# Layer 0's weight products divided as 274, 270 and 272 columns

## The chip, the cores and the metric

The kernel runs on one core of a Trainium2 chip. Its time is the device time of one launch in microseconds; the median of 3 runs of the kernel before is 2330.63 us (2329.7 to 2330.78). The profile is one execution of the same program, recorded by the hardware profiler. TensorE is called PE there (PEld is its weight load), VectorE DVE, ScalarE ACT, GpSimd POOL, SyncE SP.

## The reference

A decoder trunk of two layers, float32 throughout: 16 learned tokens and 256 input tokens make T = 272 tokens of D = 2048 features.

```python
for layer in range(2):
    a = rms_norm(h, norm_attn[layer])
    if layer == 0:
        q, k, v, f = split(a @ fox_w_in)            # 3*2048 + 16 columns
        h = h + forgetting_attention(q, k, v, cumsum(log_sigmoid(f + b_f))) @ fox_w_o
    else:
        k_s, v_s = split(rms_norm(h, kv_norm) @ w_kv)
        h = h + stick_breaking_attention(a @ sb_w_q, k_s, v_s) @ sb_w_o
    h = h + square(relu(rms_norm(h, norm_mlp[layer]) @ w_up[layer])) @ w_down[layer]
return rms_norm(h, final_norm)[:, 16:]
```

`w_up` and `w_down` are 2048 x 8192 and 8192 x 2048. Only the last 256 tokens are returned, so from layer 1's query projection on the kernel leaves out the first 16; the shared K/V projection still takes all 272.

## The kernel before

**Layout.** Features lie on the 128 partitions, tokens along the free dimension. The stream `hT` is [128, 16 chunks of features, 272 tokens] in float32.

**Precision by splitting.** A float32 product is made from rounded products (type F32R). Each weight block is split into a rounded high part `whi` (ScalarE, L222) and the rest `wlo` (VectorE, L223); each activation chunk into `hi` (L138) and `lo` (L139). A weight tile of 128 x 128 takes part in three products, whi x hi, whi x lo and wlo x hi (L253 to L255), accumulated in float32.

**Where the split activations lie.** Class `Split` (L118) takes a buffer of 16 rows, one for each chunk, of `XROW` = 640 columns, and places the two parts in each row by `ROWS` (L27): for T = 272 tokens (`t0` = 0, called layer 0 here, with the shared K/V projection) the high part at column 48 and the low part at 368; for the 256 tokens of layer 1 (`t0` = M) the high part at 304 and the low part at 0. Layer 1 reads low and high part as one operand of 2 x 256 columns (`both`, L132) in one product of 512 columns with `whi` and adds a product of 256 columns with `wlo`. 2 x 272 columns are over the 512 that one accumulator holds, so layer 0 makes three products of 272.

**The product loop.** `gemm_group` (L186) makes 512 output features from 2048 input features: four accumulators of [128, 512] in four banks (`acc`, one for each 128 output features, index m), four blocks kb of 512 input features, each in two halves hf of two tiles kc. The weights of a block are loaded in two transfers by SyncE, then split. In blocks 0 and 3 TensorE goes accumulator by accumulator, four tiles each, 12 products; in blocks 1 and 2 half by half and in it accumulator by accumulator. So a new group takes the accumulators up in the order in which the old group has finished them. The loop's products keep the order written (`gemm_matmul`, L178, pins each behind the one before, but for the first group, whose products follow the loads). The four accumulator buffers are the only ones: each must be evicted before the next group's first product on it.

**Eviction.** After block 3, `evac(m, [accumulator])` is called for each m (L258): q, k and v are scaled by the norm's factor (L376, L380); the output projection (`out_proj`) and the down projection add into `hT` (L262), the former and the last quarter of the latter also split and square the result for the next norm; the up projection makes squared ReLU and splits it (L506 to L510).

**Order.** The order on each engine is made when the program is built, by a scheduler that simulates a timeline; TensorE's is pinned as said. Small attention work of TensorE stands between the groups' products.

**Groups.** With 272 tokens: 12 for q, k, v, 4 for the output projection, 16 up, 16 down, 8 for K/V, 56 in all, of 4 x 16 weight tiles. With 256 tokens: 4, 4, 16 and 16.

Of the kernel before, what the change touches and what calls it, by code (L numbers as in the profile page):

```python
# [9 lines left out]
F32 = mybir.dt.float32  # L10
F32R = mybir.dt.float32r
AF = mybir.ActivationFunctionType
ALU = mybir.AluOpType
AX = mybir.AxisListType

P = 128
D = 2048
NC = D // P
M = 16
# [4 lines left out]
QSCALE = 1.0 / math.sqrt(P)  # L24
N_FF = 4

ROWS = {0: (48, 368), M: (304, 0)}  # L27
XROW = 640

G_A0, G_M0, G_KV, G_A1, G_M1, G_FIN = range(6)  # L30
# [3 lines left out]
def yoco_kernel(ctx: ExitStack, tc: tile.TileContext, hT_in, gains, b_f, w_f, w_qkv0, w_o0, w_up, w_dn,  # L34
                w_kv, w_q1, w_o1, outT):
    nc = tc.nc
# [7 lines left out]
    tmp = ctx.enter_context(tc.tile_pool(name="tmp", bufs=2))  # L44
# [73 lines left out]
    class Split:  # L118


        def __init__(self, label, t0):
            n = T - t0
            self.t0 = t0
            rows = xs.tile([P, NC * XROW + 64], F32R, tag="x", name=f"x_{label}")
            hi, lo = ROWS[t0]
            o = min(hi, lo)
            rows = rows[:, o:o + NC * XROW].rearrange("p (c t) -> p c t", c=NC)
            self.hi, self.lo = (rows[:, :, k - o:k - o + n] for k in (hi, lo))

            d = abs(lo - hi)  # L130
            if t0:
                self.both = rows[:, :, :2 * d].rearrange("p c (i t) -> p c i t", i=2)[:, :, :, :n]  # L132
            self.low_first = lo < hi
# [44 lines left out]
    def gemm_matmul(*args, **kw):  # L178

        ins = nc.tensor.matmul(*args, **kw).ins  # L180
        if queued and pinned[0]:
            tc.add_manual_dep(ins, queued[0].name, mybir.DependencyInfo(mybir.DependencyClass.NoSync,
                                                                        mybir.DependencyReason.DATA))
        queued[:] = [ins]

    def gemm_group(wblk, sp, t0, evac, before={}, after={}, load_x=None, pairs=False, apart=()):  # L186

        uid[0] += 1
        u = uid[0]
        accs = [pacc.tile([P, 512], F32, tag="acc", name=f"acc_{u}_{m}") for m in range(4)]
        n = T - t0
        for kb in range(4):
            src_w = wblk[kb].rearrange("p (k c) -> p k c", k=4)
            if kb in before:
                before[kb]()
            piece = 1 if load_x is not None and kb < 2 else 2  # L200
            raws = [wraw.tile([P, 2, 512], F32, tag="raw", name=f"raw_{u}_{kb}_{hf}") for hf in range(2)]
            for k0 in range(0, 4, piece):
                if load_x is not None:
                    load_x(range(4 * kb + k0, 4 * kb + k0 + piece))
                if load_x is not None and kb == k0 == 0:

                    for c0 in (0, 256):
                        nc.scalar.dma_start(raws[0][:, 0, c0:c0 + 256], src_w[:, 0, c0:c0 + 256])
                else:
                    nc.sync.dma_start(raws[k0 // 2][:, k0 % 2:k0 % 2 + piece], src_w[:, k0:k0 + piece])  # L210
            parts = []
            for hf in range(2):
                whi = wspl.tile([P, 2, 512], F32R, tag="whi", name=f"whi_{u}_{kb}_{hf}")
                wlo = wspl.tile([P, 2, 576], F32R, tag="wlo", name=f"wlo_{u}_{kb}_{hf}")
                wlo = wlo[:, :, 32:544] if pairs else wlo[:, :, :512]
                boxes = [(o, piece, 0, 512) for o in range(0, 2, piece)]
                if load_x is not None and kb == hf == 0:
                    boxes[:1] = [(0, 1, 0, 256), (0, 1, 256, 512)]
                for o, no, c0, c1 in boxes:
                    src = raws[hf][:, o:o + no, c0:c1]  # L220
                    hp, lp = whi[:, o:o + no, c0:c1], wlo[:, o:o + no, c0:c1]
                    on_act = nc.scalar.activation(hp, src, AF.Copy)  # L222
                    on_dve = nc.vector.tensor_tensor(out=lp, in0=src, in1=hp.bitcast(F32), op=ALU.subtract)  # L223
                parts.append((whi, wlo))
            if kb in after:
                with tc.issue_after(on_act.ins), tc.issue_after(on_dve.ins):
                    after[kb]()


            if load_x is not None and kb == 0:  # L230
                runs = [([kc], range(4)) for kc in range(4)]
            elif kb in (0, 3):
                runs = [(range(4), [m]) for m in range(4)]
            else:
                runs = [(range(2 * hf, 2 * hf + 2), range(4)) for hf in range(2)]
            pinned[0] = load_x is None
            for kcs, ms in runs:
                paired = [m for m in ms if pairs and m not in apart]
                single = [m for m in ms if m not in paired]
                for kc in kcs:  # L240
                    for m in paired:
                        gemm_matmul(accs[m], parts[kc // 2][0][:, kc % 2, m * P:(m + 1) * P], sp.both[:, 4 * kb + kc],
                                    start=kb == kc == 0, stop=False)
                for kc in kcs:
                    for m in paired:
                        gemm_matmul(accs[m][:, n:] if sp.low_first else accs[m][:, :n],
                                    parts[kc // 2][1][:, kc % 2, m * P:(m + 1) * P],
                                    sp.hi[:, 4 * kb + kc], start=False, stop=kb == kc == 3)
                for m in single:
                    for kc in kcs:  # L250
                        wh, wl = (w[:, kc % 2, m * P:(m + 1) * P] for w in parts[kc // 2])
                        hi, lo = sp.hi[:, 4 * kb + kc], sp.lo[:, 4 * kb + kc]
                        gemm_matmul(accs[m][:, :n], wh, hi, start=kb == kc == 0, stop=False)  # L253
                        gemm_matmul(accs[m][:, :n], wh, lo, start=False, stop=False)
                        gemm_matmul(accs[m][:, :n], wl, hi, start=False, stop=kb == kc == 3)  # L255
                if kb == 3:
                    for m in ms:
                        evac(m, [accs[m][:, :n]] + ([accs[m][:, n:]] if m in paired else []))  # L258

    def residual_add(c, acc, t0):  # L260
# [16 lines left out]
    def load_x(chunks):  # L277
        c0, n = chunks[0], len(chunks)
        nc.sync.dma_start(hT[:, c0:c0 + n, :], hT_in[:, c0:c0 + n, :])
        if c0 == 0:  # L280
            nc.sync.dma_start(g_sb, gains)
        for c in chunks:
            split_chunk(xa, G_A0, c)
# [86 lines left out]
    for g in range(4):  # L370
# [11 lines left out]
        if g == 0:  # L382

            gemm_group(w_qkv0[0], xa, 0, lambda m, acc, qT=qT: nc.scalar.copy(qT[:, m, :], acc[0]),
                       after={kb: (lambda kb=kb: first_norm(kb)) for kb in range(4)}, load_x=load_x)
            gate_products()
            box["rstd"] = norm.finish()
            for m in range(4):
                evac_q(m, [qT[:, m, :]])
            forget_gates(box["rstd"])  # L390
        else:
            gemm_group(w_qkv0[3 * g], xa, 0, evac_q)
# [4 lines left out]
        def decays(j):  # L397

            for i, (o, n) in enumerate(((0, 144), (144, T))):
                nc.vector.scalar_tensor_tensor(out=s[:, j, o:o + n], in0=fk[:, j, :n],  # L400
                                               scalar=fq_sb[:, i, 4 * g + j:4 * g + j + 1],
                                               in1=maskA[:, o:o + n], op0=ALU.subtract, op1=ALU.add)

        gemm_group(w_qkv0[3 * g + 1], xa, 0, lambda m, acc: evac_kv(m, acc, kT),
                   after={j: (lambda j=j: decays(j)) for j in range(4)})

# [31 lines left out]
        for pr in range(2):  # L438
            pp_sb = att.tile([P, 2, 416], F32, tag="pp", bufs=3, name=f"pp_sb_{g}_{pr}")
            for i in range(2):  # L440
# [14 lines left out]
                                in0=pm[:, P - M:P].unsqueeze(1).to_broadcast([P, 8, M]))  # L455
# [98 lines left out]
    for g in range(4):  # L554
# [30 lines left out]
        for pr in range(2):  # L585
# [3 lines left out]
            for i in range(2):  # L589
# [4 lines left out]
                                    in1=maskB[:, 0:256].unsqueeze(1).to_broadcast([P, 2, 256]))  # L594
            nc.vector.tensor_tensor(out=zp[:, :, 256:400], in0=pb[:, :, :144], op=ALU.add,
                                    in1=maskB[:, 256:400].unsqueeze(1).to_broadcast([P, 2, 144]))
# [15 lines left out]
            for t in (240, 384):  # L612
                nc.vector.tensor_tensor(out=zp[:, :, t:t + M], in0=zp[:, :, t:t + M],
                                        in1=sc[:, 2 * pr:2 * pr + 2, :], op=ALU.add)
# [57 lines left out]
    for i in range(2):  # L672
        pr = patt.tile([P, 512], F32, tag="patt", name=f"pr_fin_{i}")
        for b in range(2):
            nc.tensor.matmul(pr[:, b * P:(b + 1) * P], rs[:, b:b + 1].to_broadcast([P, P]), ident,
                             start=True, stop=True)
# [4 lines left out]
    for c, n in [(12, 1), (13, 1), (14, 1), (15, 1), (0, 2), (2, 2), (4, 2), (6, 2)]:  # L681
        if n == 1:
            nc.vector.scalar_tensor_tensor(out=ob[:, c, :S], in0=hT[:, c, M:], scalar=g_sb[:, G_FIN, c:c + 1],
                                           in1=prs[0], op0=ALU.mult, op1=ALU.mult)
        else:
            nc.vector.tensor_tensor(out=ob[:, c:c + n, :S], in0=hT[:, c:c + n, M:], op=ALU.mult,  # L686
                                    in1=prs[0].unsqueeze(1).to_broadcast([P, n, S]))
        nc.sync.dma_start(outT[:, c:c + n, :], ob[:, c:c + n, :S])
    for c in (8, 10):
        nc.gpsimd.tensor_tensor(out=ob[:, c:c + 2, :S], in0=hT[:, c:c + 2, M:], op=ALU.mult,  # L690
                                in1=pr_sb.unsqueeze(1).to_broadcast([P, 2, S]))
# [52 lines left out]
```

## Time and profile before

| | |
|---|---|
| median of 3 runs | 2330.63 us |
| span of the profiled execution | 2330.1 us |
| products on TensorE | 16486 |
| VectorE, ScalarE busy | 1351.1 us, 1064.1 us |
| from HBM | 407.29 MB, 176 GB/s over the span |

The head of the profile gives each engine's busy time; the chain of waits follows the work that ended last back to the start; the view of stretches gives, for a piece of the span, each engine's busy time and, in brackets, the number of its instructions; the timeline lists instructions by start, merged where neighbours are alike. A group's row reads: line, engine, operation, output <- inputs, shapes, count | busy us, mean ns of one | idle time before it.

### The profile page before, as it was taken

What the parts mean: (1) busy time and instruction counts of PE and PEld (TensorE: products, weight loads), DVE (VectorE), ACT (ScalarE), POOL (GpSimd) and SP (SyncE); (2) the same over time, 40 slices, a digit from 0 to 9 for tenths busy, and PEclk for the clock granted to TensorE, in tenths of its full rate; (3) what the DMA queues carried; (4) which work ended last, traced back from release to release, by engine and by line L of the source; (5) the groups of instructions that cost most, each with busy time, mean ns of one, the idle gap of its engine ahead of it and who ended that gap; (6) DMA issues with size and microseconds to landing.
All of it is one profiled execution on the core that took longest, in us unless ns stands there. A gap on an engine that the chain in (4) does not pass through costs nothing.

```text
span 2330.1 us, 39954 instructions
## 1 busy us (share of the span) xinstructions
PE 2317.9 (99%) x16486; PEld 2197.0 (94%) x16486; DVE 1351.1 (58%) x1923; ACT 1064.1 (46%) x1477; POOL 39.1 (2%) x58
## 2 busy tenths in 40 slices
PE   9999999999999999999999999999999999999998
PEld 9999999999999999999998999988888888888887
DVE  7665555655455455455566555567665665665665
ACT  5434344543354344344455444445544543543553
POOL 1000000000000000000000000000000000000000
PEclk9999999999999999999999999999999999999999
DMA  6445545555555555555555444455555656556563
GB/s 232 165 157 169 168 159 172 172 182 172 186 174 182 173 183 171 186 176 177 184 176 188 163 145 145 145 180 182 197 181 185 198 181 198 182 187 196 181 197 127
DMA packets 116630, 412.00 MB, mean 177 GB/s; under 512 B 13264, under 2 KB 16736, under 8 KB 116448
## 3 DMA queue, kind: packets, MB, share of 16 engines
q1 hardware_dynamic: 114560, 406.29, 52.6%
q10 hardware_dynamic: 1888, 3.16, 0.4%
q8 instruction: 129, 2.11, 0.4%
q14 instruction: 53, 0.43, 0.1%
HBM read 407.29 MB, written 2.11 MB: 176 GB/s over the span
## 4 chain that ended last, share of the span: by engine, by line
PE 99%; DMA 1%; DVE 0%; ACT 0%; issue 0%; DVEq 0%; ACTq 0%; SPq 0%
PE acc L180 95%; DMA hT<-hT_in 1%; PE ps L412 0%; PE pza L591 0%; PE pv L345 0%; PE po L474 0%; PE po L630 0%; PE pzb L592 0%; PE po L631 0%; DMA g_sb<-gains 0%; PE po L475 0%; PE po L632 0%; DVE ob L686 0%; PE pf L311 0%; PE pf L312 0%; PE pta L606 0%
## 5 line engine op out<-in xcount | busy, mean ns | idle before, releaser
L223 DVE TENSOR_TENSOR wlo<-raw,whi 128x1024 fp32r<-128x1024 f32 (+1 forms) x773 | 931.7, 1217 | 752.3 <-ACT whi L222 750.8
L222 ACT ACTIVATE whi<-raw 128x1024 fp32r<-128x1024 f32 (+1 forms) x773 | 799.0, 1050 | 960.8 <-PE acc L180 938.2
L180 PE MATMUL acc<-x_u,whi 128*128 128x272 f32 (+2 forms) x3088 | 648.2, 321 | 0.0
L180 PE MATMUL acc<-x_m,whi 128*128 128x272 f32 (+1 forms) x3072 | 646.7, 322 | 0.0
L180 PEld LDWEIGHTS acc<-x_u,whi 128*128 128x128 f32 x3088 | 500.5, 188 | 26.5
L180 PEld LDWEIGHTS acc<-x_m,whi 128*128 128x128 f32 x3072 | 498.6, 188 | 27.2
L180 PE MATMUL acc<-x_u,wlo 128*128 128x272 f32 (+1 forms) x2048 | 448.1, 284 | 0.0
L180 PE MATMUL acc<-x_m,wlo 128*128 128x272 f32 (+1 forms) x2048 | 446.0, 284 | 0.0
L180 PE MATMUL acc<-x_a,whi 128*128 128x272 f32 (+1 forms) x1792 | 361.1, 306 | 1.4 <-ACT whi L222 1.2
L180 PEld LDWEIGHTS acc<-x_u,wlo 128*128 128x128 f32 x2048 | 342.1, 188 | 16.2
L180 PEld LDWEIGHTS acc<-x_m,wlo 128*128 128x128 f32 x2048 | 341.4, 188 | 16.4
L180 PEld LDWEIGHTS acc<-x_a,whi 128*128 128x128 f32 x1792 | 284.7, 189 | 10.7 <-ACT whi L222 1.6
L180 PE MATMUL acc<-x_a,wlo 128*128 128x272 f32 (+1 forms) x1024 | 255.1, 287 | 0.0
L180 PE MATMUL acc<-x_kv,whi 128*128 128x272 f32 x1024 | 194.1, 288 | 0.0
L180 PEld LDWEIGHTS acc<-x_a,wlo 128*128 128x128 f32 x1024 | 180.1, 188 | 5.0 <-issue 0.5
L180 PE MATMUL acc<-x_o,whi 128*128 128x272 f32 (+1 forms) x768 | 162.5, 322 | 0.0
L180 PEld LDWEIGHTS acc<-x_kv,whi 128*128 128x128 f32 x1024 | 160.6, 188 | 0.4
L180 PE MATMUL acc<-x_kv,wlo 128*128 128x272 f32 x512 | 147.3, 288 | 0.0
L262 DVE TENSOR_TENSOR hT<-acc,hT 128x256 f32<-128x256 f32 (+1 forms) x239 | 102.5, 429 | 72.0 <-PE acc L180 70.1
L180 PEld LDWEIGHTS acc<-x_o,whi 128*128 128x128 f32 x768 | 124.4, 188 | 6.7
L180 PE MATMUL acc<-x_o,wlo 128*128 128x272 f32 (+1 forms) x512 | 112.1, 284 | 0.0
L180 PEld LDWEIGHTS acc<-x_kv,wlo 128*128 128x128 f32 x512 | 96.5, 188 | 0.1
(226 smaller groups left out, 1040.2 us busy)
## 6 DMA issues: line engine op xcount, KB each, us to landing
raw<-w_up SPq DMA_DIRECT2D x256, 512.0 KB, 4.7
raw<-w_dn SPq DMA_DIRECT2D x256, 512.0 KB, 4.8
raw<-w_qkv SPq DMA_DIRECT2D x92, 512.0 KB, 3.8
raw<-w_o SPq DMA_DIRECT2D x64, 512.0 KB, 4.5
raw<-w_kv SPq DMA_DIRECT2D x64, 512.0 KB, 3.7
raw<-w_q SPq DMA_DIRECT2D x32, 512.0 KB, 4.6
fk<-f_dram ACTq DMA_DIRECT2D x4, 544.0 KB, 4.8
raw<-w_qkv SPq DMA_DIRECT2D x7, 256.0 KB, 4.5
```

The lines of the kernel that those rows point to most:

```text
L180: ins = nc.tensor.matmul(*args, **kw).ins
L222: on_act = nc.scalar.activation(hp, src, AF.Copy)
L223: on_dve = nc.vector.tensor_tensor(out=lp, in0=src, in1=hp.bitcast(F32), op=ALU.subtract)
L262: nc.vector.tensor_tensor(out=hT[:, c, t0:], in0=a, in1=hT[:, c, t0:], op=ALU.add)
```

## The change

In layer 0 the high and low parts of a chunk are put side by side, columns 48 to 320 and 320 to 592 of a row. The view `last_lo` begins two columns ahead of the low part, so it holds the high part of the last two tokens and then the low part of all 272. The three products of a weight tile become:

- whi x `last_lo`, 274 columns, into columns 0 to 274 of the accumulator,
- whi x the high part of the first 270 tokens, into columns 2 to 272,
- wlo x the high part of all 272 tokens, into columns 2 to 274.

Columns 2 to 274 then hold the tokens, and columns 0 and 1 the product of `whi` with the high part of the last two tokens. At eviction these two columns are copied by ScalarE to a small tile `over` and added by VectorE to columns 272 and 273, in place, before `evac` gets columns 2 to 274.

```diff
-ROWS = {0: (48, 368), M: (304, 0)}
+ROWS = {0: (48, 320), M: (304, 0)}
+OVER = 2
...
+            if not t0:
+                self.last_lo = rows[:, :, n - OVER:2 * n]
...
-                        gemm_matmul(accs[m][:, :n], wh, hi, start=kb == kc == 0, stop=False)
-                        gemm_matmul(accs[m][:, :n], wh, lo, start=False, stop=False)
-                        gemm_matmul(accs[m][:, :n], wl, hi, start=False, stop=kb == kc == 3)
+                        if t0 == 0:
+                            gemm_matmul(accs[m][:, :OVER + n], wh, sp.last_lo[:, 4 * kb + kc],
+                                        start=kb == kc == 0, stop=False)
+                            gemm_matmul(accs[m][:, OVER:n], wh, hi[:, :n - OVER], start=False, stop=False)
+                            gemm_matmul(accs[m][:, OVER:OVER + n], wl, hi, start=False, stop=kb == kc == 3)
+                        else:
...
                 if kb == 3:
                     for m in ms:
+                        if t0 == 0:
+                            last = accs[m][:, n:n + OVER]
+                            over = tmp.tile([P, OVER], F32, tag="over", name=f"over_{u}_{m}")
+                            nc.scalar.copy(over, accs[m][:, :OVER])
+                            nc.vector.tensor_tensor(out=last, in0=last, in1=over, op=ALU.add)
+                            evac(m, [accs[m][:, OVER:OVER + n]])
+                            continue
```

The `else` branch holds the three products of before, for layer 1.

More of the change, by code (lines that the diff above doesn't have):

```diff
@@ L252, in gemm_group @@
                         hi, lo = sp.hi[:, 4 * kb + kc], sp.lo[:, 4 * kb + kc]
-                        gemm_matmul(accs[m][:, :n], wh, hi, start=kb == kc == 0, stop=False)
-                        gemm_matmul(accs[m][:, :n], wh, lo, start=False, stop=False)
-                        gemm_matmul(accs[m][:, :n], wl, hi, start=False, stop=kb == kc == 3)
+                        if t0 == 0:
[4 more added lines that the diff above has]
+                        else:
+                            gemm_matmul(accs[m][:, :n], wh, hi, start=kb == kc == 0, stop=False)
+                            gemm_matmul(accs[m][:, :n], wh, lo, start=False, stop=False)
+                            gemm_matmul(accs[m][:, :n], wl, hi, start=False, stop=kb == kc == 3)
                 if kb == 3:
                     for m in ms:
+                        if t0 == 0:
[5 more added lines that the diff above has]
+                            continue
                         evac(m, [accs[m][:, :n]] + ([accs[m][:, n:]] if m in paired else []))
```

## The prediction

> **What bounds the kernel now.** I read the head of the profile first, then its chain of waits, then what TensorE waited for, then stretches of the span.
>
> ```profile
> span 2330.1 us, 39954 instructions
> PE 2317.9 (99%) x16486; PEld 2197.0 (94%) x16486; DVE 1351.1 (58%) x1923; ACT 1064.1 (46%) x1477; POOL 39.1 (2%) x58
> ...
> PE 99%; DMA 1%; DVE 0%; ACT 0%; issue 0%; DVEq 0%; ACTq 0%; SPq 0%
> ```
>
> 99% of the chain that ends last is TensorE. The other engines matter only where they make TensorE wait. How often that is, the view of TensorE's waits says (who waited for whom: total us, times, longest):
>
> ```profile
> PE pr_fin L675 <- DVE fin L669: 1.3, 1, 1.3
> PE acc L180 <- ACT whi L222: 1.2, 2, 0.9
> PE idle L61 <- DVE mean_w L57: 1.1, 1, 1.1
> ```
>
> These are the costliest three, and they come to under 4 us. So the time is the number of products times the distance between the starts of two of them. "Busy" means little here (a busy engine may still be slow), hence the view of stretches, which counts the products that start in each:
>
> ```profile
> core 0: us, PE busy (x) PEld busy (x) DVE busy (x) ACT busy (x) POOL busy (x), PEclk, DMA share, GB/s
> 444.00:1190.00 746.00, 746.00 (x6049) 745.95 (x6048) 389.16 (x475) 320.73 (x411) 0.00 (x0) 1.00 0.54 178
> ```
>
> From 444 to 1190 us layer 0 runs nothing but 272-column products at full granted clock (PEclk 1.00): 746 us / 6049 = 123.33 ns each, 370.0 ns for the three of one weight tile, 0.4534 ns a column. No wait interrupts them. The number of weight tiles that the change touches is the number of `wlo` products of 272 columns, in the view of groups with shapes kept apart:
>
> ```profile
> L180 PE MATMUL acc<-x_m,wlo 128*128 128x272 f32 x1024 | 293.4, 287 | 0.0
> L180 PE MATMUL acc<-x_u,wlo 128*128 128x272 f32 x1024 | 293.4, 286 | 0.0
> L180 PE MATMUL acc<-x_a,wlo 128*128 128x272 f32 x768 | 216.9, 289 | 0.0
> L180 PE MATMUL acc<-x_kv,wlo 128*128 128x272 f32 x512 | 147.3, 288 | 0.0
> L180 PE MATMUL acc<-x_o,wlo 128*128 128x272 f32 x256 | 73.6, 288 | 0.0
> ```
>
> 1024 + 1024 + 768 + 512 + 256 = 3584 tiles (the shared K/V projection is among them), 3584 × 0.370 = 1326 us of the span. One ns more or less per tile is 3.6 us, 0.15%. (The 287 ns in these rows is one product from start to end; products overlap, so it is not the pace.)
>
> **The change, part by part.**
>
> *Products.* Three products stay three, with a weight load each, and 274 + 270 + 272 = 816 columns are as many as 3 × 272. If a column costs the same wherever it stands, the pace stays at 370.0 ns. It need not. The first product now starts two columns ahead of a chunk's low part, at column 318 of its row, where every stream of before starts at a multiple of 16 columns (48, 368, 304, 0); two of the three outputs start at column 2 of their bank; the low part moves up against the high part. The trace has no such product, so I bound the price per column by other rows. Layer 1 alternates products of 512 columns (two pieces of 256, a gap between them) with products of 256. First its usual pace, then a stretch of its last group, both from the timeline (start us, us, engine, line):
>
> ```profile
> 1606.62 2.01 PE L180 MATMUL acc<-x_m,whi 128*128 128x512 f32 x8
> 1608.47 1.11 PE L180 MATMUL acc<-x_m,wlo 128*128 128x256 f32 x8
> 1609.41 2.01 PE L180 MATMUL acc<-x_m,whi 128*128 128x512 f32 x8
> ...
> 2308.08 1.53 PE L180 MATMUL acc<-x_u,whi 128*128 128x512 f32 x6
> 2309.45 0.84 PE L180 MATMUL acc<-x_u,wlo 128*128 128x256 f32 x6
> 2310.12 0.28 PE L180 MATMUL acc<-x_u,whi 128*128 128x256 f32 x1
> ```
>
> 8 × (512 + 256) = 6144 columns in 1609.41 − 1606.62 = 2.79 us is 0.4541 ns a column; 6 × 768 = 4608 columns in 2310.12 − 2308.08 = 2.04 us is 0.4427. The same shapes run at two paces, so columns alone don't set it. The dearest row is in layer 1's attention, products of the same rounded type read in two pieces each:
>
> ```profile
> 1335.46 0.40 PE L607 MATMUL pta<-el,ntri_r 128*128 128x512 f32 x1
> 1335.69 0.29 PE L608 MATMUL pta<-eh,nones_r 128*128 128x288 f32 x1
> 1335.83 0.30 PE L609 MATMUL pta<-el,nones_r 128*128 128x288 f32 x1
> 1335.96 0.29 PE L611 MATMUL ptb<-el,ntri_r 128*128 128x288 f32 x1
> 1336.09 0.41 PE L180 MATMUL acc<-x_kv,whi 128*128 128x272 f32 x2
> ```
>
> 512 + 3 × 288 = 1376 columns in 0.63 us: 0.4578 ns a column. For 816 columns the three prices give 361.2, 370.5 and 373.6 ns against 370.0: −31 us, +2 us and +13 us over 3584 tiles. The new first product is in substance a scrap of 2 columns and a run of 272, nearest to the rows that read two pieces, so I take the middle of the two dearer ones: 0.45595 × 816 = 372.1 ns, +2.1 ns a tile, **+7.3 us**. The ends stay −31 and +13.
>
> The Trainium skill ("SBUF — State Buffer", Door 1: The DMA port swizzle) says that SBUF has 16-byte lines and that each access that crosses to a new line pays something; it names no price. Column 318 lies 8 bytes past such a line, so by that rule the first product touches one line more than 272 aligned columns and the sum goes up, never down; no run here shows it.
>
> *Eviction.* 56 groups × 4 accumulators get one copy on ScalarE and one add on VectorE, 128x2 each. Ops of that size stand in the final normalisation:
>
> ```profile
> L664 ACT ACTIVATE fin<-fin 128x2 f32<-128x2 f32 x1 | 0.2, 204 | 0.9 <-DVE fin L663 0.9
> L667 DVE TENSOR_TENSOR fin<-fin 128x2 f32<-128x2 f32 x1 | 0.2, 160 | 0.5 <-ACT fin L665 0.5
> ```
>
> 224 × 0.204 = 46 us of ScalarE and 224 × 0.160 = 36 us of VectorE, on engines that are 46% and 58% busy. They are free while each accumulator is evicted before TensorE wants it again. Accumulator m is wanted 36 products after its last one (three accumulators of 12 products lie between), 36 × 0.1233 = 4.44 us later. The tightest is the fourth. In the changed program its copy stands behind both splits `whi` of the next block on ScalarE; on VectorE its add stands behind both `wlo`, and in the groups that also feed a norm (four of the output projection) its eviction behind one correction and one sum of squares as well. The timeline of a group with norm work in the kernel before:
>
> ```profile
> 1117.92 1.06 ACT L222 ACTIVATE whi<-raw 128x1024 fp32r<-128x1024 f32 x1 [0.84 <-ACT sq_a L155]
> 1118.74 0.44 DVE L262 TENSOR_TENSOR hT<-acc,hT 128x272 f32<-128x272 f32 x1 [0.69 <-PE acc L180]
> 1119.61 1.04 ACT L222 ACTIVATE whi<-raw 128x1024 fp32r<-128x1024 f32 x1
> 1120.23 0.48 DVE L139 SCALAR_TENSOR_TENSOR x_a<-hT,g_sb,x_a 128x256 fp32r<-128x256 f32 x1
> 1120.62 0.44 DVE L156 TENSOR_TENSOR ssq_a<-ssq_a,sq_a 128x272 f32<-128x272 f32 x1
> 1120.98 1.22 DVE L223 TENSOR_TENSOR wlo<-raw,whi 128x1024 fp32r<-128x1024 f32 x1
> ```
>
> The accumulator is done at 1118.74 (the add that waited for it starts). In the new order ScalarE ends its splits at 1117.92 + 1.06 + 1.04 = 1120.02 and the copy at 1120.22; VectorE ends the second `wlo` at 1121.24, the small add at 1121.40, correction and squares at 1122.32, the add into `hT` at 1122.76. Wanted at 1118.74 + 4.44 = 1123.18: 0.4 us to spare. Taken at **0**; if another split slipped in front (1.05 us), TensorE would stand for 0.6 us in such a group. The next work behind the copy on ScalarE is the splits of block 2, wanted only 5.9 us after block 1 begins.
>
> *Dependencies.* The first product of a chunk now needs the low part too, which VectorE writes 0.48 us (row L139) after the high part. In the steady groups chunks are ready many microseconds early. At the very start it may cost up to 0.5 us; TensorE waits there again later for `whi` (1.2 us, above), which absorbs part: **+0.2**. SyncE's and GpSimd's instructions and the transfers keep their order, so nothing is moved past them.
>
> Sum: 7.3 + 0 + 0.2 = +7.5 us on the execution's 2330.1, 2337.6. The median of the runs, 2330.63, lies 0.5 above that span: forecast **2338 us**, +0.3%.
>
> **The rivals.**
>
> *A cheaper middle product (faster).* At layer 1's quick rate 272 columns would take 120.4 ns; they take 123.33, in 6049 of them without change. So each product ends with some 2.9 ns of lost time, and time lost so evenly may come in steps. If 270 columns fall below a step and 274 stay on theirs, the middle product costs 270 × 0.4427 = 119.5 ns and the tile 3.8 ns less: −13.7 us, **2317**; if the new pattern moves all three to the quick pace, −31 us, 2300. For it: the two paces of the same shapes. Against it: layer 0 never shows the quick pace in 746 us, and 274 may as well step up.
>
> *A column is a column (no change).* 370.0 ns as before, **2331**. For it: equal sums, equal loads, and 0.4534 against 0.4541 for different shapes. Against it: the spread 0.4427 to 0.4578. The Trainium skill ("TensorE: Matmul & The Clock Gate", Back-to-back issue gap) has a rule of this kind: columns at 2.4 GHz plus 2.5 ns, so 274 and 270 together cost what twice 272 cost. It gives 115.8 ns for 272 columns; the trace shows 123.33, so something that the rule leaves out is at work.
>
> *Late accumulators (much slower).* If the copies come behind one more split in the 24 groups with the most eviction work (4 output projection, 16 up, 4 last down), 24 × 0.6 = 14 us on top of the forecast: **2352**. It decides from 0.4 us of added delay on. Against it: the margin above; and 3 of 4 accumulators have more.
>
> **How the numbers follow.** Forecast 0.39, cheaper middle product 0.33, no change 0.15, late accumulators 0.13. A difference of 0.2%, 4.7 us, is about what a measurement of this kernel tells from none. Faster by more: 0.33 and 0.02 of the no-change case, 0.35. Slower by more: 0.13 and 0.34 of the forecast (its low end, +2 us, doesn't count), 0.47. Between: 0.18. The forecast's own range is 2333 to 2345 (bounds +2 and +13). The range for 8 in 10 reaches into both sides: down to 2309, which leaves out the far part of the quick pace (about 0.1), up to 2352.
>
> **What would show it.** Steps: the stretch in layer 0's MLP holds 746 us / 3 × tile price; 372 ns a tile would be 6015 products in 746 us. Under 370 the first rival is right, at 370.0 the second. The tile's three distances show which product changed: the forecast wants the first one longer than 124.2 (274 columns at the old 0.4534), the others within 1 ns of theirs. Late accumulators would show as waits of TensorE for VectorE at groups' starts; the forecast wants none above 1 us. Layer 1 apart from K/V must keep its pace. I am wrong if a tile costs under 370, or if such waits sum to more than 3 us.

## The result and the profile after

The changed kernel takes 2354.52 us (median of 4 runs, 2353.27 to 2356.84) against 2330.41 us on the same chip: a ratio of 1.0105, 95% interval 1.0092 to 1.0117, or +24.1 us. The forecast was 2338, its range ended at 2352.

The head of the profile, instructions and busy time of each engine:

```profile
span 2354.0 us, 40567 instructions
PE 2334.7 (99%) x16486; PEld 2212.0 (94%) x16486; DVE 1384.1 (59%) x2147; ACT 1089.9 (46%) x1701; POOL 17.6 (1%) x58
```

As many products as before and 224 instructions more on each of VectorE and ScalarE; TensorE still has 99%. The stretch in layer 0's MLP, with the same columns as before (us, then busy time of each engine and, in brackets, the instructions that run in the stretch, granted clock, DMA share, GB/s):

```profile
core 0: us, PE busy (x) PEld busy (x) DVE busy (x) ACT busy (x) POOL busy (x), PEclk, DMA share, GB/s
444.00:1190.00 746.00, 746.00 (x5995) 745.92 (x5994) 406.12 (x592) 332.44 (x529) 0.00 (x0) 1.00 0.53 177
```

5995 products where 6049 had run (in both, two of them began ahead of the stretch): 746 / 5995 = 124.44 ns each, 373.3 ns a tile against 370.0, at full granted clock and without a wait. But the K/V projection runs slower still. Two rows of its timeline (start, duration, engine, line):

```profile
1298.07 0.42 PE L183 MATMUL acc<-x_kv,whi 128*128 128x274 f32 x2
...
1301.12 0.29 PE L183 MATMUL acc<-x_kv,whi 128*128 128x274 f32 x1
```

Eight tiles lie between these starts: 3.05 us / 8 = 381 ns a tile, within the rounding of the 380.0 that the whole group gives, whose tiles run without an interruption. Between attention's products the K/V groups run either at 380.0 or at about 373.4; in 6 of the 8 groups most tiles are at 380.0. The other 50 groups have means of 373.3 to 375.2 (the first 376.3); the kernel before has 370.0 to 370.4 in all 56.

The second part of the loss are waits. TensorE's view of them (who waited for whom: total us, times, longest):

```profile
PE acc L183 <- DVE z L629: 4.9, 4, 1.4
PE ps L428 <- DVE kT L396: 1.7, 1, 1.7
PE pr_fin L691 <- DVE fin L685: 1.3, 1, 1.3
PE idle L62 <- DVE mean_w L58: 1.1, 1, 1.1
PE acc L183 <- DVE qT L392: 1.0, 3, 0.3
PE acc L183 <- DVE x_a L142: 0.9, 2, 0.7
```

The rows for `z`, `kT` and `qT` are new, 7.6 us. One of the four long ones, first on ScalarE, then on VectorE, then on TensorE:

```profile
1347.54 0.86 ACT L579 ACTIVATE e<-e 128x800 f32<-128x800 f32 x1
1348.30 0.86 ACT L633 ACTIVATE z<-z 128x800 f32<-128x800 f32 x1
1349.06 1.04 ACT L225 ACTIVATE whi<-raw 128x1024 fp32r<-128x1024 f32 x1
1350.01 0.14 ACT L270 COPY over<-acc 128x2 f32<-128x2 f32 x1
```

```profile
1350.14 1.23 DVE L226 TENSOR_TENSOR wlo<-raw,whi 128x1024 fp32r<-128x1024 f32 x1 [1.24 <-ACT over L270]
1351.28 0.16 DVE L271 TENSOR_TENSOR acc<-acc,over 128x2 f32<-128x2 f32 x1
1351.35 0.98 DVE L581 SCALAR_TENSOR_TENSOR e<-z,e 128x800 f32<-128x800 f32 x1
1352.25 0.43 DVE L396 TENSOR_TENSOR vT<-acc,rstd_a 128x272 f32<-128x272 f32 x1
1352.60 0.28 DVE L629 TENSOR_TENSOR z<-z,sc 128x32 f32<-128x32 f32 x2
```

```profile
1351.39 0.29 PE L183 MATMUL acc<-x_kv,wlo 128*128 128x272 f32 x1
1352.83 0.48 PE L183 MATMUL acc<-x_kv,whi 128*128 128x274 f32 x2 [1.14 <-DVE z L629]
```

The copy of 0.14 us comes behind three long operations on ScalarE, two of them layer 1's attention, which runs beside the K/V groups. The small add comes behind a `wlo` on VectorE, and the eviction `vT`, the last reader of the accumulator, behind one more attention operation. It ends at 1352.68, and TensorE goes on at 1352.83, 1.44 us after its last product's start. The profile names `z`, the neighbour that came last on VectorE; the reader of the accumulator is `vT`.

The wait for `kT` is made elsewhere. Its copy, its small add, its eviction and the product that waited:

```profile
61.62 0.14 ACT L270 COPY over<-acc 128x2 f32<-128x2 f32 x1
67.66 0.15 DVE L271 TENSOR_TENSOR acc<-acc,over 128x2 f32<-128x2 f32 x1
68.39 0.41 DVE L396 TENSOR_TENSOR kT<-acc,rstd_a 128x272 f32<-128x272 f32 x1
68.86 0.97 PE L428 MATMUL ps<-kT,qT 128*128 128x144 f32 x4 [1.71 <-DVE kT L396]
```

The copy was done at 61.76 us; the add comes 5.9 us later, because the order that the scheduler made for VectorE has attention's operations and two `wlo` ahead of it. The shorter waits for `qT` look alike: there the add comes 2.3 us behind the copy.

Where the 23.9 us of span come from: take for each of the 56 groups the mean distance of its tiles, from the starts in the trace, less that of the kernel before, times 64 tiles. That makes 14.4 us of pace: 3.0 in the q, k and v groups, 0.9 in the output projection, 6.9 in the MLP and 3.7 in the K/V groups. It leaves 9.5 us, of which the rows above show 7.6 as waits. Another part is the clock of this one execution, right behind the wait for `kT`. The same stretch, first in the changed kernel, then in e2_evict (below), which has that wait too:

```profile
70.00:73.70 3.70, 3.70 (x18) 3.58 (x17) 2.98 (x12) 3.02 (x10) 0.00 (x0) 0.54 0.26 103
70.00:73.70 3.70, 3.70 (x31) 3.69 (x31) 3.40 (x13) 3.44 (x10) 0.00 (x0) 1.00 0.27 100
```

At a granted clock of 0.54 instead of 1.00 there are 13 products fewer; at 0.123 us each that is some 1.6 us, an estimate. Two of the changed kernel's four runs, at 2355.7 and 2356.8 us, have the mean clock of this execution, 0.997, and the other two, at 2353.3 and 2353.4 us, have 0.998 as the kernel before has. On the other side the profile before holds 1.2 us of waiting for `whi` at its start that the changed kernel's doesn't. So 9.5 us is a remainder and no exact price of the evictions; e2_evict measures them alone.

Layer 1 apart from K/V keeps its pace: over its query projection the difference between the kernels stays at 14.1 us, and from the end of its output projection on at 23.4 to 23.9 us.

### The profile page after: what moved, and what is told of

It reads as the page before. It is cut to its first block, busy times and chain, and to the rows that moved or that the text cites. A ratio compares the mean times of both kernels' runs of the same rounds, so it can differ in the third digit from the quotient of the medians.

```text
span 2354.0 us, 40567 instructions
## 1 busy us (share of the span) xinstructions
PE 2334.7 (99%) x16486; PEld 2212.0 (94%) x16486; DVE 1384.1 (59%) x2147; ACT 1089.9 (46%) x1701; POOL 17.6 (1%) x58
## 4 chain that ended last, share of the span: by engine, by line
PE 86%; DVE 1%; ACT 1%; issue 0%; DVEq 0%; ACTq 0%
PE acc L183 84%; PE pza L607 0%; PE po L646 0%; PE pv L361 0%; ACT whi L225 0%; DVE wlo L226 0%; PE po L647 0%; DVE e L581 0%; ACT e L579 0%; ACT z L633 0%; PE pzb L608 0%; PE ps L428 0%; DVE z L609 0%; PE po L648 0%; DVE ob L702 0%
## 5 line engine op out<-in xcount | busy, mean ns | idle before, releaser
L183 PE MATMUL acc<-x_u,whi 128*128 128x274 f32 (+3 forms) x3088 | 651.7, 321 | 0.0
L183 PE MATMUL acc<-x_m,whi 128*128 128x274 f32 (+2 forms) x3072 | 650.1, 322 | 0.0
L183 PE MATMUL acc<-x_a,whi 128*128 128x274 f32 (+2 forms) x1792 | 361.0, 306 | 1.9 <-DVE qT L392 1.0
L183 PE MATMUL acc<-x_kv,whi 128*128 128x274 f32 (+1 forms) x1024 | 197.3, 289 | 3.5 <-DVE z L629 3.5
L183 PE MATMUL acc<-x_o,whi 128*128 128x274 f32 (+2 forms) x768 | 163.4, 323 | 1.4 <-DVE z L629 1.4
L270 ACT COPY over<-acc 128x2 f32<-128x2 f32 x224 | 34.3, 154 | 155.6 <-PE acc L183 149.8
```

Of the source, the lines that this page charges most:

```text
L270: nc.scalar.copy(over, accs[m][:, :OVER])
```

## The experiments

Times are medians beside runs of the kernel before on the same chip, whose median was 2330.2 to 2330.8; the last two are single executions, beside one of 2329.08 us. "Tile" is the mean distance from one tile's first product to the next one's, within groups and where nothing stands between the tiles, from the starts in the traces.

| run | us | ratio, 95% interval | tile, ns |
|---|---|---|---|
| e1_layout | 2342.57 | 1.0052, 1.0036 to 1.0069 | 373.3 |
| e2_evict | 2340.92 | 1.0045, 1.0030 to 1.0060 | 370.0 |
| e3_products | 2347.30 | 1.0073, 1.0058 to 1.0088 | 373.4 in MLP, mixed with 380.0 elsewhere |
| e4_outshift | 2330.40 | 1.0000, 0.9991 to 1.0010 | 370.0 |
| f1_both0 | 2359.25 | 1.0125, 1.0096 to 1.0155 | 380.0 in MLP, 376.0 elsewhere |
| f2_gap64 | 2342.38 | 1.0051, 1.0028 to 1.0074 | 373.3 |
| f3_both32 | 2365.73 | 1.0153, 1.0124 to 1.0183 | 380.0 |
| f4_lo352 | 2342.37 | 1.0052, 1.0029 to 1.0074 | 373.2 |
| g1_over16 | 2352.02 | 1.0092, 1.0076 to 1.0107 | 373.4 |
| g2_evict_dve | 2331.40 | 1.0003, 0.9994 to 1.0012 | 370.0 |
| g3_both16 | 2364.09 | 1.0143, 1.0122 to 1.0163 | 380.0 |
| g4_m48 | 2330.69 | 1.0000, 0.9990 to 1.0010 | 370.0 |
| g5_m0 | 2335.99 | 1.0024, 1.0014 to 1.0034 | 370.0 |
| h1_from50 | 2345.05 | 1.0062, 1.0042 to 1.0082 | 374.2 |
| h2_to318 | 2343.04 | 1.0053, 1.0033 to 1.0074 | 372.9, K/V partly 380.0 |
| h3_after_dve | 2356.92 | 1.0112, 1.0095 to 1.0129 | 373.4 before the MLP, 380.0 in it |
| i1_kick_after | 2354.58 | | 373.4 and 380.0 in turn |
| i2_kick_before | 2338.93 | | 370.0, behind eight of the small products 380.0 |

### The parts of the change, one by one

**e1_layout**: the kernel before with the parts side by side, nothing else.

```diff
-ROWS = {0: (48, 368), M: (304, 0)}
+ROWS = {0: (48, 320), M: (304, 0)}
```

> Only the low part moves, from column 368 to 320; products, outputs and eviction are those of before. Theory (the first product's start two columns ahead of a multiple of 16 sets the new pace): 370.0 ns a weight tile, time within 2 us of before. Rival (the place of the low part sets it): 373.4 ns a tile in the MLP and 380 in the K/V groups, +12 us and more.

The instructions and their order on every engine are those of before; only addresses differ. Its stretch in the MLP:

```profile
444.00:1190.00 746.00, 746.00 (x5995) 745.92 (x5995) 384.29 (x466) 317.97 (x404) 0.00 (x0) 1.00 0.54 177
```

5995 products, as in the changed kernel. So this pace needs neither the products of 274 and 270 columns nor the start two columns ahead: moving the low part alone gives as much, and my theory fell. (That the same thing slows the changed kernel is likely but not shown: the three products of a tile share the loss out differently there, as the distances further down say.)

**e4_outshift**: only the outputs move, by two columns.

```diff
+                        z = 0 if t0 else 2
-                        gemm_matmul(accs[m][:, :n], wh, hi, ...
+                        gemm_matmul(accs[m][:, z:z + n], wh, hi, ...
```

> Layout, operands and counts of before; all three products write columns 2 to 274 of their bank instead of 0 to 272. Theory (operand start): 370.0 ns a tile, within 2 us of before. Rival (outputs off the bank's start cost): above 371 ns a tile, +4 us or more.

No difference; the outputs' place costs nothing here.

**e2_evict**: the kernel before with a copy on ScalarE and a small operation on VectorE ahead of each eviction.

```diff
+                            nc.scalar.copy(over, accs[m][:, :2])
+                            nc.vector.scalar_tensor_tensor(out=last, in0=over, scalar=0.0, in1=last,
+                                                           op0=ALU.mult, op1=ALU.add)
```

> Products and layout of before; at each of the 224 evictions a copy of two accumulator columns on ScalarE and an op on two columns on VectorE that adds 0 times that copy, so the result stays that of before. Theory (the part of the loss that is not pace, some 11 us, comes from the evictions and the order they bring): pace 370.0 ns a tile, time +4 to +12 us, lost in the q, k, v groups and the K/V groups. Rival (the evictions are hidden, all the loss is pace): within 2 us of before.

+10.4 us at an unchanged pace. TensorE's waits:

```profile
PE acc L180 <- DVE z L619: 5.2, 4, 1.5
PE ps L418 <- DVE kT L386: 1.8, 1, 1.8
PE pr_fin L681 <- DVE fin L675: 1.3, 1, 1.3
PE acc L180 <- DVE qT L382: 1.2, 3, 0.4
```

These are the changed kernel's new rows, with the same counts and nearly the same sizes. Layer 0's MLP, with 32 of the 56 groups, adds nothing: it starts and ends 2.7 us behind the kernel before, and some 6 us more arise by the end of layer 1's output projection.

**g2_evict_dve**: the same with the copy on VectorE, in front of the small operation.

```diff
-                            nc.scalar.copy(over, accs[m][:, :2])
+                            nc.vector.tensor_copy(over, accs[m][:, :2])
```

> Kernel before with the two small ops at each eviction, as in the run with the evictions alone, but the copy too on VectorE, so that no eviction stands behind ScalarE's queue. Theory (the loss is the accumulator waiting for its copy behind ScalarE's attention and split work): 370.0 ns a tile, under +5 us instead of +10. Rival (any op more at the evictions makes the scheduler place them late): +8 us or more, with the same stalls of 1.5 us at the ends of the K/V groups.

```profile
PE pr_fin L681 <- DVE fin L675: 1.3, 1, 1.3
PE idle L61 <- DVE mean_w L57: 1.1, 1, 1.1
PE acc L180 <- DVE x_o L373: 0.8, 1, 0.8
```

In the view of TensorE's waits the rows for `z`, `kT` and `qT` are gone, and with them the loss (a wait of 0.8 us, for `x_o`, is new). Two small operations per eviction cost nothing that can be measured; that one of them stands in ScalarE's queue, with the order that the scheduler then makes, costs 9.5 us (2340.92 against 2331.40, beside kernels before of 2330.49 and 2330.81).

**e3_products**: the changed kernel without the copy and the small add.

```diff
-                            nc.scalar.copy(over, accs[m][:, :OVER])
-                            nc.vector.tensor_tensor(out=last, in0=last, in1=over, op=ALU.add)
```

> The changed kernel without the copy and the add at eviction: the product of the high weights with the last two tokens' high parts is left out of the result. Theory (pace from the products, the rest from the evictions): 373.4 ns a tile in the MLP, 380 ns in the K/V groups as in the changed kernel, time +12 to +17 us on before, that is 7 to 12 us under the changed kernel. Rival (evictions hidden): as the changed kernel, +24 us.

None of the waits for `z`, `kT` and `qT` remains, yet it is +16.8 us, where 56 groups at 373.3 would be 11.8: the output projection, six of the K/V groups and six of q, k and v run wholly or mostly at 380.0.

### What of the place sets the pace

All of these change columns of rows in the kernel before; each engine's instructions and their order stay as they were.

```diff
-ROWS = {0: (48, 368), M: (304, 0)}
+ROWS = {0: (48, 384), M: (304, 0)}    (f2_gap64)
+ROWS = {0: (48, 352), M: (304, 0)}    (f4_lo352)
+ROWS = {0: (0, 320), M: (304, 0)}     (f1_both0)
+ROWS = {0: (32, 352), M: (304, 0)}    (f3_both32)
+ROWS = {0: (16, 336), M: (304, 0)}    (g3_both16)
+ROWS = {0: (48, 368), M: (368, 48)}   (g4_m48)
+ROWS = {0: (48, 368), M: (320, 0)}    (g5_m0)
```

> Kernel before with the low part at column 384: a gap of 64 columns to the high part, and a start at a multiple of 64, as in the run with the low part at 320. Theory (start modulo 64): 373.4 ns a tile, +12 us. Rival (the missing gap): 370.0 ns, within 2 us of before.

> Kernel before with the low part at column 352: starts of 48 and 32 modulo 64, a gap of 32. Theory (both parts starting alike modulo 64 is what gives 370.0, unlike starts cost): about 373 ns a tile. Rival (only the missing gap, or only a start at a multiple of 64, costs): 370.0.

> Kernel before with the high part at column 0 and the low part at 320 of a row; nothing else changes. Theory (the pace depends on where streams start modulo 64 columns, 256 bytes; before, both start at 48 modulo 64): another pace than 370.0 ns a tile; if a start at a multiple of 64 is what costs, 377 ns, 3.4 ns more for each part that starts there, +24 us. Rival (a part that lies against the other, without a gap, costs): 370.0, since a gap of 48 stands here as before.

> Kernel before with the high part at column 32 and the low part at 352, both 32 modulo 64, the gap of 48 kept. Theory (start modulo 64): a pace of its own, between 361 and 377 ns a tile. Rival (the gap): 370.0.

> Kernel before with the parts at columns 16 and 336, both 16 modulo 64. With starts of 0 and of 32 the tile took 376.5 to 380 ns, with 48 370.0. Theory (only 48, where 272 columns end at a multiple of 64, is cheap): 376 to 380 ns, +24 to +35 us. Rival (every second multiple of 16 is cheap): 370.0.

With a gap between the parts wider than before (384) or narrower (352) the tile stays at 373.3 and 373.2, so it is not the missing gap. Moving the high part as well makes it worse. The stretch in the MLP of f3_both32:

```profile
444.00:1190.00 746.00, 746.00 (x5890) 745.92 (x5889) 375.26 (x450) 311.65 (x392) 0.00 (x0) 1.00 0.53 174
```

746 / 5890 × 3 = 380.0 ns. From the starts in the trace, each of the three products has gone from 123.3 to 126.6 ns there. In e1_layout they take 125.8, 124.2 and 123.3. The tiles found are of 370.0, 373.3, 376.0 and 380.0 ns. f1_both0 shows two of them on one layout: 376.0 up to the products of the norm at 446.6 us, 380.0 behind them to the end of the MLP, 376.0 again in the K/V groups. The Trainium skill ("SBUF — State Buffer", Door 1: The DMA port swizzle) has an access pay at each 16-byte line; all parts in these layouts start at a multiple of 4 columns of 4 bytes, and the tiles yet differ by 10 ns a tile, so this rule doesn't explain the differences.

> Kernel before with layer 1's parts moved: high part at column 368, low part at 48, both 48 modulo 64 (before: 304 and 0). Layer 0 untouched. Theory carried over (start modulo 64 sets the pace): layer 1's pair of products, 349.5 ns before, changes, if 48 is cheap there too to some 341 to 346 ns, 3.5 to 8.5 ns on 2560 pairs, -9 to -22 us. Rival (256 columns have no cheap start): the same or slower.

> Kernel before with layer 1's high part at column 320 instead of 304 (low part at 0 as before): in layer 1 all streams of 256 start and end at multiples of 64. Theory (the end at a multiple of 64 is cheap): layer 1's pair of products under 349.5 ns, down to 341, 0 to -22 us. Rival (256 columns are not helped, as with both parts at 48): within 2 us of before, or slower.

For layer 1's 256 columns these two places gain nothing: the one is the same, the other 5.8 us slower.

**g1_over16**: the changed kernel with OVER = 16, so that the first product has 288 columns from 304 on and the second 256.

```diff
-OVER = 2
+OVER = 16
```

> The changed kernel with 16 columns carried over instead of 2: products of 288, 256 and 272 columns, which start at columns 304, 48 and 48 of a row, all 48 modulo 64. Theory (the start modulo 64 sets the pace, not the division): 370 ns a tile, and of the change's +24 us only the evictions' part is left, +10 to +12 us on before. Rival (the division costs, or where a stream ends): 373 ns a tile or more, +22 us or more.

All starts were then as in the kernel before by their distance from a multiple of 64 columns, and the tile took 373.4: with products of 288, 256 and 272 columns, that start alone doesn't bring 370.0. The waits were the changed kernel's (4.9, 1.7 and 1.1 us for `z`, `kT` and `qT`).

**h1_from50, h2_to318**: the kernel before with products of 270 columns, from column 50 on or up to 318, but for a group's first tile; so nearly all of the sum for two tokens is left out.

```diff
+                        i, k = (0, n) if t0 or kb == kc == 0 else (2, n)        (h1_from50)
+                        i, k = (0, n) if t0 or kb == kc == 0 else (0, n - 2)    (h2_to318)
-                        gemm_matmul(accs[m][:, :n], wh, hi, ...
+                        gemm_matmul(accs[m][:, i:k], wh, hi[:, i:k], ...
```

> Kernel before, but in every weight tile except a group's first the three products take only the last 270 tokens: the first two tokens are left out there. Streams start at 50 modulo 64 and end, as before, at a multiple of 64. Theory (the end at a multiple of 64 makes 370.0 cheap, the start doesn't matter): 367 to 370 ns a tile, 0 to -10 us. Rival (the start at 48 makes it cheap): 373 to 380 ns, +12 to +35 us.

> As the run that starts at 50, but the last two tokens are left out instead: streams start at 48 modulo 64, as before, and end at 62. Theory (the end decides): 373 to 380 ns a tile although two columns fewer, +10 to +35 us. Rival (the start decides): 367 to 370 ns, 0 to -10 us.

Both are slower than before with 0.7% fewer columns: in the MLP's stretch 6002 products run in h2_to318, 5980 in h1_from50, 6049 with 272 columns. So neither the end nor the start alone brings 370.0. Each of these runs is one order of products, though, and the next experiments show that one layout can have two paces: what they compare are layouts under that order.

### The same products at two paces

**h3_after_dve**: the changed kernel with the copy on VectorE.

```diff
-                            nc.scalar.copy(over, accs[m][:, :OVER])
+                            nc.vector.tensor_copy(over, accs[m][:, :OVER])
```

> The changed kernel with the copy of the two columns on VectorE instead of ScalarE. Theory (the loss is the sum of pace and evictions behind ScalarE): the pace part alone is left, 373.4 ns a tile (380 where it falls into that pace), +12 to +17 us on before instead of +24. Rival (the two parts are not separate): above +20 us.

+26.7 us, far from the 12 to 17 expected. The waits are gone (none on an accumulator is over 0.8 us), and layer 0's MLP starts 3.1 us behind the kernel before, where the changed kernel was 7.3 behind. But the MLP ends 23.3 behind. Stretches ahead of it, at its start and in it:

```profile
360.00:440.00 80.00, 80.00 (x645) 80.00 (x644) 52.84 (x102) 40.04 (x59) 0.00 (x0) 1.00 0.54 175
450.00:530.00 80.00, 80.00 (x634) 80.00 (x633) 45.92 (x82) 37.74 (x53) 0.00 (x0) 1.00 0.53 173
530.00:1190.00 660.00, 660.00 (x5213) 660.00 (x5212) 362.47 (x616) 275.82 (x341) 0.00 (x0) 1.00 0.53 173
```

Without the two or three products that began ahead of each stretch, that is 374 ns a tile, then 380 and 380: the same products on the same layout. The step lies at one place of TensorE's timeline:

```profile
446.23 0.28 PE L183 MATMUL acc<-x_m,wlo 128*128 128x272 f32 x1
446.35 0.62 PE L164 MATMUL pms_m<-ssq_m,mean_w 128*128 128x272 f32 x2
446.61 0.62 PE L183 MATMUL acc<-x_m,whi 128*128 128x274 f32 x2
```

Two products of the norm stand between two tiles. The tiles ahead of them follow at 373.4 ns, those behind at 380.0, for the 766 us to the end of the MLP, in which nothing interrupts them. In the changed kernel the norm's products come at 450.6, behind other tiles, and the pace stays 373.4. What follows one interruption makes 13 us of the MLP (20.3 us over the kernel before, where the changed kernel has 6.9).

**i1_kick_after, i2_kick_before**: one further small product in each of layer 0's MLP groups, in the kernel of h3_after_dve and in the kernel before.

```diff
+            if t0 == 0 and kb == 1 and 17 <= u <= 48:
+                w = 16 * (1 + u % 8)
+                ps = patt.tile([P, 512], F32, tag="patt", name=f"kick_{u}")
+                gemm_matmul(ps[:, :w], parts[0][0][:, 0, :P], sp.hi[:, 4, :w], start=True, stop=True)
```

> The changed kernel with the small copy on VectorE (h3_after_dve), and in each of the 32 groups of layer 0's MLP one further small product (16 to 128 columns, its result unused) ahead of block 1. In h3_after_dve the tile goes from 373.5 to 380.0 ns at the two products of the norm at 446.4 us and stays there for 740 us. Theory (several paces are open to the same products, and whatever stands between two tiles sets which one follows, until the next interruption): after the small products some groups run at 373.5 and others at 380, changing only at such a product; the 32 groups are mixed, and the time is anywhere between 2342 and 2361. Rival (the pace belongs to the place of the data in this program): all 32 groups stay at 380.0 and the time grows by the small products alone, about 32 x 0.06 us = 2 us, to 2359.

> The kernel before with the same 32 small products. Theory (with the streams of the kernel before only one pace is open): 370.0 ns a tile in all groups, about +2 to +4 us, 2333 to 2335. Rival (every layout has several paces, and the kernel before has been in its quick one by its order alone): some groups go to 373 or 380, and the time passes 2337.

Four stretches of i1_kick_after, each between two small products:

```profile
466.00:484.00 18.00, 18.00 (x145) 18.00 (x144) 10.03 (x21) 8.70 (x12) 0.00 (x0) 1.00 0.54 176
490.00:508.00 18.00, 18.00 (x147) 18.00 (x146) 10.36 (x20) 8.55 (x12) 0.00 (x0) 1.00 0.53 176
514.00:532.00 18.00, 18.00 (x144) 18.00 (x143) 10.03 (x20) 8.30 (x11) 0.00 (x0) 1.00 0.53 177
538.00:556.00 18.00, 18.00 (x147) 18.00 (x147) 9.62 (x18) 6.25 (x6) 0.00 (x0) 1.00 0.54 176
```

Two or three of the products in brackets began ahead of the stretch, so 142, 144, 142 and 145 start there. 380 ns a tile makes 142.1 in 18 us, 373.4 makes 144.6. Over the whole way from one small product to the next the tiles take 380.0, 373.3, 380.0 and 373.4 ns, and the pace turns at every one of the small products from 463.6 us to the last. The theory held. Whether each product flips the pace or its length picks it isn't separated, since the lengths alternate too: from 463.6 us on 380.0 follows those of 16, 48, 80 and 112 columns, about 373.4 those of 32, 64, 96 and 128. Only the first product, of 32 columns at 439.0 us, is followed by 380.0 (until the norm's products at 445.2 turn it back) and speaks against the length alone. And two neighbouring stretches of i2_kick_before:

```profile
580.00:598.00 18.00, 18.00 (x148) 18.00 (x147) 8.78 (x10) 6.38 (x8) 0.00 (x0) 1.00 0.54 181
606.00:624.00 18.00, 18.00 (x144) 18.00 (x144) 8.37 (x11) 6.27 (x6) 0.00 (x0) 1.00 0.54 176
```

They run at 370.0 and 380.0 ns a tile, on the kernel before's own layout. The first small product, of 32 columns, brings 380.0 until the norm's products 6 us later. Then seven of the products, all of 16 or 48 columns, bring 380.0, and all but the last of these stretches end at the next small product, of 32 or 64; the first product of 48 columns, and all of 80 to 128, changed nothing. The same 48 columns, met at 370.0, changed nothing once and brought 380.0 three times, so the length alone doesn't decide here either. So here the rival was right: the layout of before has a slow pace too, and its own order of products doesn't meet it.

## Why the prediction was wrong

*Evictions.* The step "Taken at **0**" failed: they cost 10.4 us in e2_evict, by themselves, and most of the 9.5 us that the pace leaves of the changed kernel's span. The new waits, 7.6 us, are also over the 3 us that the prediction named as a sign of being wrong. Its prices were fair (0.204 and 0.160 us a piece, measured 0.154 and 0.163 on average), and in the output projection and the MLP, where its margin of 0.4 us was worked out, TensorE shows no wait for an eviction. What failed was the choice of place: I took the groups with norm work to be the tightest because VectorE has most to do there, and didn't lay the two operations into the queues of the groups beside which attention runs. In the K/V groups the copy stands in ScalarE's queue, where attention's operations of 0.86 us stand among the splits (4.9 us in four waits, all with the order of rows shown above); in the q and k groups the add stands late in VectorE's (2.7 us). There the accumulator's eviction had depended on VectorE alone, and the copy bound it to a second queue. That g2_evict_dve loses nothing shows that the copy's place on ScalarE makes the loss; how it divides between the two queues is read from the rows. The rival of late accumulators had the mechanism, a copy behind one operation too many, but put it in 24 groups of output projection and MLP, where nothing was late.

*Pace.* The term of +7.3 us was mis-sized and its reason was wrong. 372.1 ns was forecast, 373.3 measured (+11.8 us over 3584 tiles), and 380.0 in most tiles of six groups brings it to 14.4. The scrap of two columns at column 318 isn't needed for it: e1_layout has no scrap and the same pace. The forecast wanted the first product longer than 124.2 ns and the others within 1 ns of theirs; on average in the MLP it is 125.0, 122.1 and 126.3 ns from their starts to the next, against 123.4, 123.3 and 123.3 before. The product that nobody touched, `wlo` x high part, is 3.0 ns longer by that. I priced each product by itself from rows of other shapes, and the time is a property of the run of products: of where the streams lie, and of what stood between the tiles. That 6049 products had one even distance was read as a price; it was one of several paces.

*Dependency.* +0.2 us at the start is of the right size, but the runs don't settle it: the five kernels with the new dependency start their first product at 5.7 to 6.2 us, the others at 5.0 to 5.8, and the first group's length scatters by more than that (25.0 to 27.4 us between its first and last product).

*The rivals of the products.* A cheaper middle product: it became 1.2 ns shorter, about what two columns are worth, and the third gave more back; no quick pace came. "A column is a column" fails in e1_layout, with equal columns and 3.3 ns more a tile; only moving the outputs (e4_outshift) was free. Its rule from the Trainium skill ("TensorE: Matmul & The Clock Gate", Back-to-back issue gap), which the page gives for an isolated product, knows only the number of columns; f3_both32 with the instructions of before and 10 ns more a tile shows that this number isn't enough here.

*The range.* It ended where the late accumulators alone would end. Both terms, 14.4 us and some 9 to 10, went the same way, and I had no case in which a dearer pace and late evictions come together.

Open stays why there are several paces, what in the position of a stream sets them (under the orders that were run, start, end and gap are each ruled out as the only cause), and which interruptions turn them. A version of the changed kernel without the waits and at 373.4 ns throughout would, by the tiles alone, still stand some 12 us behind the kernel before; none that was run is ahead of it.

## What to carry to other kernels

A small operation added to an eviction was priced here by where it stands in the engines' queues, not by its length: keep it on the engine that evicts anyway, and look for the tightest group where another stage's work shares that engine. The saturated run of products here has a pace that is not a sum of column prices; when a change moves operands or puts something between the products, read the distance of starts group by group, and expect up to some 3% from the place alone (380.0 against 370.0 ns). So test the new layout by itself, with the old instructions, before building on it.

## What was not expected of the hardware

With the same instructions in the same order at full granted clock, the column at which the two parts of a chunk start changes the pace from 370.0 to 373.3, 376.0 or 380.0 ns a tile, up to 35 us of the kernel (f3_both32). With the same layout, a single product of 48 columns between two tiles can change it by 6.6 ns a tile (373.4 to 380.0, i1_kick_after) or 10 ns (370.0 to 380.0, i2_kick_before), and the pace then holds until the next interruption, for 766 us in h3_after_dve.
